# Which matrix products of a decoder block run as seven-product pairs, and which one runs beside the attention

## The chip, the cores and the metric

The kernel runs on one core of a Trainium2 chip. The metric is the device time of one execution in microseconds (us). Three runs of the kernel before gave a median of 1796.05 us (1795.31 to 1798.83). One further execution, 1795.55 us long, was recorded by the hardware profiler; every duration below comes from its trace.

## The reference

One layer of a hybrid decoder with S = 1024 tokens and D = 1024 channels, in float32. The parts that the change touches:

```
mod = silu(c) @ w_ada + b_ada                      # six rows of 1024: sh1, sc1, g1, sh2, sc2, g2
h = rms_norm(x, pre_norm1_w) * (1 + sc1) + sh1
z, xbc, dt_raw, q, k, v, gates = split(h @ w_in)   # 1024, 1536, 16, 1024, 1024, 1024, 2048 columns
y = ssd_chunked(silu(conv(xbc)), dt, ...) + d_skip * xs
y = y * silu(z)
y_ssd = y * rsqrt(mean of y*y over each of 2 groups of 512 channels + eps) * norm_w
q, k = partial_rope(q), partial_rope(k)            # 16 of each 64 channels are rotated by position
y_att = rms_norm(softmax1 @ v - lam * softmax2 @ v) per head, for 8 heads of 128 channels
gate_ssd, gate_att = split(sigmoid(gates))
merged = gate_ssd * (y_ssd @ w_ssd_o) + gate_att * (y_att @ w_attn_o)
x = x + g1 * rms_norm(merged @ w_out)
u = conv(h2 @ w_up);  x = x + g2 * rms_norm((gelu(u_gate) * u_val) @ w_down)
```

## The kernel before, in words

Everything is kept transposed, channels on the 128 partitions and tokens along the free axis. A float32 matrix product is done as three reduced-precision products: each operand is split into a high part (a copy on ScalarE, ACT) and a low part (the difference, on VectorE, DVE), and TensorE (PE) adds high·high, high·low and low·high. A *block* is 128 output channels of a projection for all 1024 tokens; with 8 slices of the input channels, 2 halves of the tokens and 3 products it takes 48 matmuls with a moving tile of 128x512.

Two blocks can also be made as a *pair*: the two blocks and the two halves of the tokens and of the input channels form a 2x2 product of matrices, done with seven products of sums instead of eight (`order`, `x_mms`, `x_split`, `x_sum`). A pair takes 7 x 4 x 3 = 84 matmuls where two blocks take 96. Its seven products gather in the PSUM banks X, Y, Z; DVE reads these into the result tiles `cg` and `cv` (`xcg`, `xcv` in the trace), and the work on a finished pair (`post(m, step)`) is laid over the time of the next pair by the table `steps_at`: at most one step after each of its seven products. Its weights arrive with `x_load` (SP's queue) in three buffers.

In the manual schedules the order of instructions on PE, DVE, ACT and SP is the order in which the code is written. SP issues nearly all the DMAs. The stages, in order:

1. The head: h, the first blocks of `xbc` and the first four blocks of gates.
2. The pairs loop: 13 pairs, listed in `pairs`: 2 of gates (`gs`, for gate_ssd), 6 that hold one q and one k block each (`qk` 2 to 7, heads that need no rotation in this layout), 5 of `xbc`. In the two pairs after the first, ten of the adaLN products are summed (`ada_sum`: DVE multiplies a 128x1024 tile of w_ada with silu(c) and sums along the row; three buffers `adas`).
3. z, also with seven products; six more `ada_sum`.
4. The SSD stage, units u = 0 to 15 of chunked recurrence; the blocks of v run between them as a dense stream (`fill`).
5. A stage called `seq`: four full blocks with rotation (`w_q` 0, `w_k` 0, `w_q` 1, `w_k` 1; `rope` does the rotation) and the eight blocks of the SSD output product (`w_ssd_o`; `so_half`, `so_out`), which also multiplies by the row `rsr` of 1/rms and by the gate. In the cover of this stage lie the split of y into `yT` (`split_y`), three `ada_sum`, and the differences of w_down that a later seven-product stage needs (`down_sum`, DVE, for k < KSO).
6. Attention: 64 items (8 heads j, 8 query blocks i). PE computes scores, transposes and values of an item; DVE the maxima, reciprocal and probabilities; ACT the exponentials. Item t's `transposes` on PE wait for its `probs` on DVE. To keep PE busy between, a dense stream is spread over the items by `fill(quota)`: 128 steps of three matmuls, the 8 blocks of gate_att (`gap`, tanh on ACT, a store to `gad`). `norm_o` normalises four query blocks of a head: POOL squares (`osb`), DVE reduces and scales (`sqt`), POOL takes the power -0.5 of `sqt` (`rstd_of`), DVE multiplies, POOL scales `osb`.
7. The attention output product, with the remaining `ada_sum`; `merged @ w_out`; the FFN up and down products.

The lists that set which blocks are made where:

```
pairs = [("gs", 4, 5), ("gs", 6, 7)] + [("qk", b, b) for b in range(2, 8)] + [("xbc", b, b + 1) for b in range(2, 12, 2)]
steps_at = {"gs": {0: (0,), 1: (4,)}, "qk": {0: (0, 1), 2: (4, 5)}, "xbc": {0: (0,), ..., 6: (7,)}}
seq = [("w_q", 0), ("w_k", 0), ("w_q", 1), ("w_k", 1)] + [("w_ssd_o", j) for j in range(8)] + [("w_gate", 8), ("w_gate", 9)]
```

## Time and profile before

| what | value |
|---|---|
| median of three runs | 1796.05 us (1795.31 to 1798.83) |
| the profiled execution | 1795.55 us, of which the span of the trace is 1793.8 us |
| PE busy | 1763.5 us, 98% of the span, 8563 matmuls |
| DVE, ACT, POOL busy | 1335.8 us (74%), 916.9 us (51%), 184.5 us (10%) |
| granted clock of PE | 0.999 |
| pairs loop | about 97 to 343 us |
| z | to about 395 us |
| SSD stage with v | 395 to 568 us |
| `seq` stage | 568 to 699 us |
| attention with the gate_att blocks | 699 to 959 us |

The lists of the profile are read so: a group of instructions has its line in the kernel, engine, operation, output and inputs by the program's names, shapes, count, then busy time in all and the mean of one in ns, then the idle time of that engine ahead of them and what ended it. A list of windows gives for each stretch the busy time and count on every engine, then the granted clock as a share of full speed, the busy share of the DMA engines and GB/s. A line of a timeline gives the start and the duration of one instruction, and in brackets how long its engine had been idle and who ended that.

### The profile page before, as it was taken

Reading aid. Unit: us, or ns where it says so; the run is one execution under the profiler, and the core shown is the slowest. Engines: PE = TensorE matmul, PEld = TensorE weight load, DVE = VectorE, ACT = ScalarE, POOL = GpSimd, SP = SyncE. Lnnn points to the kernel's source line nnn. Section 1 sums busy time; section 2 is a strip of 40 time slices with the busy share of each in tenths; the row PEclk is TensorE's granted clock in tenths of the full one; section 3 lists DMA queues with packets and bytes.
Section 4 is the critical chain, followed back from the end, with each engine's and each line's share of the span. In section 5 each row is a group of like instructions: output and inputs, shape, how many; then the busy total and the mean of one; then the engine's idle time right before and its main releaser. Section 6 shows DMA issues by size and latency. Waiting matters only on the chain.

```text
span 1793.8 us, 23879 instructions
## 1 busy us (share of the span) xinstructions
PE 1763.5 (98%) x8563; PEld 1456.3 (81%) x8563; DVE 1335.8 (74%) x2042; ACT 916.9 (51%) x1642; POOL 184.5 (10%) x189
## 2 busy tenths in 40 slices
PE   7999999999999999999999999999999999999998
PEld 4788888888878888888887888888888888888887
DVE  7887568864777787878876876688898888876545
ACT  7654445547765302666665232665454544554532
POOL 0000000002551300112122103100000000000001
PEclk9999999999999999999999999999999999999999
DMA  9465653356657798775728979212332232378744
GB/s 376 188 212 160 190 145 106 118 202 215 208 188 259 181 334 257 201 201 141 188 77 292 322 263 348 106 64 107 115 122 93 100 112 100 127 246 294 255 151 159
DMA packets 148330, 337.29 MB, mean 188 GB/s; under 512 B 15570, under 2 KB 50290, under 8 KB 148212
## 3 DMA queue, kind: packets, MB, share of 16 engines
q1 hardware_dynamic: 145012, 325.28, 55.4%
q0 software_dynamic: 3200, 10.49, 1.5%
q8 instruction: 67, 1.10, 0.3%
q14 instruction: 51, 0.42, 0.1%
HBM read 240.46 MB, written 95.25 MB: 187 GB/s over the span
## 4 chain that ended last, share of the span: by engine, by line
PE 56%; DVE 8%; DMA 3%; ACT 2%; issue 2%; POOL 1%; SPq 1%; DVEq 0%; POOLq 0%; ACTq 0%
PE upx L2043 4%; PE upx L2042 4%; PE upx L2044 4%; PE o L1700 2%; PE upy L2043 2%; PE upy L2042 2%; PE upy L2044 2%; PE dx L2438 2%; PE dx L2439 2%; PE dx L2437 2%; PE dy L2438 2%; PE dy L2437 2%; PE dy L2439 2%; PE mix L2116 2%; PE mix L2117 2%
## 5 line engine op out<-in xcount | busy, mean ns | idle before, releaser
L2042 PE MATMUL upx<-t,wu_t 128*128 128x512 f32 x264 | 103.1, 391 | 0.5 <-DVE cv L2502 0.4
L2043 PE MATMUL upx<-t,wu_t 128*128 128x512 f32 x264 | 102.8, 390 | 0.2 <-DVE t L2173 0.2
L2044 PE MATMUL upx<-t,wu_t 128*128 128x512 f32 x264 | 102.7, 389 | 0.0
L2016 ACT ACTIVATE wu_t<-sab 128x512 fp32r<-128x512 f32 x57 | 34.1, 627 | 127.7 <-DVE sab L2033 127.7
L102 DVE TENSOR_TENSOR g_lo<-gst,g_hi 128x1024 fp32r<-128x1024 f32 (+1 forms) x42 | 47.6, 1135 | 50.5 <-ACT g_hi L101 50.3
L1659 DVE CUSTOM_DVE_ANT_0 sc<-sc,mstrip 128x640 f32<-128x640 f32 (+3 forms) x64 | 65.9, 1029 | 14.4 <-PE sc L1626 13.9
L1671 ACT ACTIVATE p<-sc,nmx 128x640 f32<-128x640 f32 (+3 forms) x64 | 61.6, 962 | 28.3 <-DVE nmx L1659 24.6
L101 ACT ACTIVATE g_hi<-gst 128x1024 fp32r<-128x1024 f32 (+1 forms) x42 | 41.5, 989 | 67.0 <-DMA gst<-gld_s 35.4
L1700 PE MATMUL o<-vt,aT 128*128 128x128 f32 x576 | 74.8, 275 | 0.0
L1625 PE MATMUL sc<-kst,qst 128*128 128x512 f32 (+3 forms) x192 | 70.7, 373 | 2.9 <-ACT p L1671 2.6
L1700 PEld LDWEIGHTS o<-vt,aT 128*128 128x128 f32 x576 | 69.3, 192 | 0.6
L2561 POOL TENSOR_TENSOR rsf<-rsf,nhalf 128x1 f32<-128x1 f32 x8 | 5.2, 656 | 623.8 <-DVE rsf L2560 623.8
L1626 PE MATMUL sc<-klo,qst 128*128 128x512 f32 (+3 forms) x192 | 63.8, 341 | 0.0
L546 PE MATMUL xx<-xt,xw_t 128*128 128x512 f32 x156 | 61.0, 391 | 0.1
L2060 DVE SCALAR_TENSOR_TENSOR ug<-cg,vec,ug 128x1023 f32<-128x1023 f32 (+1 forms) x44 | 56.3, 1280 | 6.1 <-ACT ug L2059 5.3
L547 PE MATMUL xx<-xt,xw_t 128*128 128x512 f32 x156 | 60.7, 389 | 0.0
L548 PE MATMUL xx<-xt,xw_t 128*128 128x512 f32 x156 | 60.7, 389 | 0.0
L1690 ACT COPY aT<-at 128x512 f32<-128x512 f32 (+2 forms) x96 | 42.8, 482 | 33.3 <-PE at L1689 33.1
L2020 DVE TENSOR_TENSOR wu_t<-sab,wu_t 128x512 fp32r<-128x512 f32 x57 | 39.3, 690 | 26.6 <-ACT wu_t L2016 26.6
L2042 PEld LDWEIGHTS upx<-t,wu_t 128*128 128x128 f32 x264 | 49.6, 188 | 11.8 <-DVE cv L2502 1.4
L521 ACT ACTIVATE xw_t<-xsab 128x512 fp32r<-128x512 f32 x39 | 23.7, 627 | 67.5 <-DVE xsab L530 66.9
L2043 PEld LDWEIGHTS upx<-t,wu_t 128*128 128x128 f32 x264 | 49.6, 188 | 10.6 <-DVE t L2173 0.5
(580 smaller groups left out, 5735.6 us busy)
## 6 DMA issues: line engine op xcount, KB each, us to landing
adas<-in_w_ada SPq DMA_DIRECT2D x32, 512.0 KB
wuf<-in_w_up SPq DMA_DIRECT2D x22, 512.0 KB
gld_s<-gsum SPq DMA_DIRECT2D x22, 512.0 KB
gst<-gld_s SPq DMA_DIRECT2D x20, 512.0 KB
wdt_raw<-wtd SPq DMA_DIRECT2D x20, 512.0 KB
wuv<-in_w_up SPq DMA_DIRECT2D x19, 512.0 KB
gld_a<-ug SPq DMA_DIRECT2D x33, 256.0 KB
adat<-in_w_ada SPq DMA_DIRECT2D x16, 512.0 KB
```

The source lines that it names most:

```text
L546: T.matmul(o, wh, xh_, start=(k == 0 and first), stop=False, skip_group_check=not first)
L1625: T.matmul(sc, qs_[s][:, tsl], ks_[s][:, n0:n1], start=True, stop=False)
L1626: T.matmul(sc, qs_[s][:, tsl], kl[s][:, n0:n1], start=False, stop=True)
L1659: V.tensor_tensor_reduce(out=sc, in0=sc, in1=strip, scale=-1.0, scalar=BIG, op0=ALU.add, op1=ALU.min, accum_out=nmx[bq][s][:, 0:1])
L1671: A.activation(p.rearrange("p (h t) -> p h t", h=2) if i == 4 else p, sc, AF.Exp, scale=-1.0, bias=nmx[bq][s][:, 0:1], accum_out=ssum[bq][ ...
L1700: T.matmul(po_of[j, grp][:, qi, :], aTs[t % 2][:, kt // 4, kt % 4, :], vt[j % 2][:, kt, :], start=(kt == 0), stop=(kt == i))
L2042: T.matmul(out_, wh, xh_, start=(k == 0 and first), stop=False, skip_group_check=not first)
L2043: T.matmul(out_, wh, xl_, start=False, stop=False, skip_group_check=not first)
L2044: T.matmul(out_, wl, xh_, start=False, stop=(k == end), skip_group_check=not first)
L2437: T.matmul(o, gh[:, kk, tsl], wh, start=(k == 0 and not more), stop=False, skip_group_check=more)
L2438: T.matmul(o, gh[:, kk, tsl], wl, start=False, stop=False, skip_group_check=more)
L2439: T.matmul(o, gl[:, kk, tsl], wh, start=False, stop=(k == KF - 1), skip_group_check=more)
```

## The change

All sixteen gate blocks but the first four, and the rotated q and k blocks 0 and 1, become pairs: the list has 19 pairs instead of 13. The `seq` stage goes. The eight SSD output blocks become the dense stream of the attention, in place of the gate_att blocks, in 16 half blocks of 8 steps (128 steps as before); at each end ACT copies the bank, POOL multiplies by the loaded gate (`gtl`) and adds, and SP stores. The row `rsr` is now multiplied into y ahead of the split, on POOL (`scale_y`); half 0 of y is split at the end of the SSD stage, half 1 in the attention's items 5, 7, 9 and 11. All 32 `ada_sum` lie in the pairs (four in each gate pair but the first, two in each qk pair), in place and with two buffers. The first four k of `down_sum` go to POOL in attention items 16 to 47. The rotation's multiplication by `ropc` stays on POOL.

```diff
-    pairs = [("gs", 4, 5), ("gs", 6, 7)] + [("qk", b, b) for b in range(2, 8)] + [("xbc", b, b + 1) for b in range(2, 12, 2)]
+    pairs = [("gate", b, b + 1) for b in range(4, 16, 2)] + [("qk", b, b) for b in range(2, 8)] + [("rope", b, b) for b in range(2)] + [("xbc", b, b + 1) for b in range(2, 12, 2)]
...
+        elif kind == "rope":
+            w_ = ("w_q", "w_k")[n]
+            ropc, rops, sw, *his = rope_t
+            hi = his[n].bitcast(F32R)
+            if step % 4 == 0:
+                A.activation(c_, c_, AF.Copy, scale=qscale[w_])
+                V.stream_shuffle(sw, c_, perm)
+            elif step % 4 == 1:
+                G.tensor_tensor(c_, c_, ropc, op=ALU.mult)
+                V.tensor_tensor(sw, sw, rops, op=ALU.mult)
+            elif step % 4 == 2:
+                V.tensor_tensor(c_, c_, sw, op=ALU.add)
+                A.activation(hi, c_, AF.Copy)
+            else:
+                lo = c_.bitcast(F32R)
+                V.tensor_tensor(lo, c_, hi.bitcast(F32), op=ALU.subtract)
+                store_qk(w_, b, hi, lo)
...
+    steps_at = {"gate": {0: (0,), 1: (4,)}, ..., "rope": {0: (0,), 1: (1,), 2: (2,), 3: (3, 4), 4: (5,), 5: (6,), 6: (7,)}, "xbc": {...}}
...
-                    adas = [SL.get(f"adas{i}") for i in range(3)]
+                    adas = [SL.get(f"adas{i}") for i in range(2)]
...
-                if p < {1: 5, 2: 5}.get(m, 0):
-                    ada_sum(n_ald < 10)
+                if n_ada < 32 and p in {"gate": (1, 2, 3, 4), "qk": (1, 4)}.get(kind, ()) and m > 0:
+                    ada_sum()
...
+    def scale_y(half, kp):
+        t = yr_of[half, kp]
+        G.tensor_tensor(t, t, rsr[:, kp // 2 : kp // 2 + 1, :].broadcast_to([P, 2, HALF]), op=ALU.mult)
...
-    blocks = list(range(8))
+    blocks = [(j, 0) for j in range(4)] + [(j, 1) for j in range(4)] + [(j, h) for j in range(4, KD) for h in range(2)]
...
-                A.activation(gev[:, half, :], ps, AF.Tanh, scale=0.5)
-                SP.dma_start(gad[j][:, half * HALF : (half + 1) * HALF], gev[:, half, :])
+            e, g_ = gev[:, n % 2, :], gtl[:, n % 2, :]
+            A.copy(e, ps)
+            G.tensor_tensor(g_, g_, e, op=ALU.mult)
+            G.tensor_tensor(e, e, g_, op=ALU.add)
+            SP.dma_start(msd[j][:, hsl], e)
...
+            if t == 0:
+                norm_sums(ps_wc("norms")[:, : 2 * P], 1)
...
+            elif t == 2:
+                norm_rstd(1)
+                norm_row(1)
+            elif 4 <= t < 12:
+                kp = (t - 4) // 2
+                if t % 2 == 0:
+                    scale_y(1, kp)
+                else:
+                    for k in (2 * kp, 2 * kp + 1):
+                        split_y(k, 1)
...
+            elif 16 <= t < 48:
...
+                elif n in (3, 4, 5, 6):
+                    down_sum(wdr, k, n - 3, SP, G)
```

**The start of the attention.** On DVE the last rows of `so_out` (the gate times the SSD output) stood ahead of the first maxima (`sc`, `nmx`) before:

```order
L1461 TENSOR_TENSOR sev<-so_1_5658,rsr_5026 128x512 [waits DVE_49,PE_49]
L1461 TENSOR_TENSOR sev<-so_1_5658,rsr_5027 128x512
L1462 TENSOR_TENSOR sev<-sev 128x512 [waits DVE_49]
L1463 SCALAR_TENSOR_TENSOR gth_5071<-gth_5071,sev 128x512 [waits DVE_49]
L1653 TENSOR_TENSOR sc_0_0_5742<-sc_0_0_5742,maskneg 128x2x128 [waits PE_49]
L1654 TENSOR_REDUCE nmx_0_5711<-sc_0_0_5742 128x2 [waits DVE_49]
L1653 TENSOR_TENSOR sc_1_0_5747<-sc_1_0_5747,maskneg 128x2x128 [waits PE_49]
L1654 TENSOR_REDUCE nmx_0_5713<-sc_1_0_5747 128x2 [waits DVE_49]
```
Now the end of the SSD stage stands there: the last `tt` and `yt` of the recurrence, four splits of y (`yT`), the product of `yt` with silu(z) and the sum of squares, then the maxima, the first probabilities (`p`) and the low part of the weights of the dense stream's second block (`so_lo`):

```order
L1251 TENSOR_TENSOR tt<-po_1_5569,eb 128x512 [waits PE_49]
L1256 TENSOR_TENSOR yt_4286<-py_1_5575,yt_4286 128x512 [waits PE_49]
L1334 SCALAR_TENSOR_TENSOR yT_0_5594<-yr_5208,vec,yT_0_5594 128x512 [waits Activation_49]
L1334 SCALAR_TENSOR_TENSOR yT_0_5597<-yr_5208,vec,yT_0_5597 128x512 [waits Activation_49]
L1334 SCALAR_TENSOR_TENSOR yT_0_5600<-yr_5209,vec,yT_0_5600 128x512 [waits Activation_49]
L1334 SCALAR_TENSOR_TENSOR yT_0_5603<-yr_5209,vec,yT_0_5603 128x512 [waits Activation_49]
L1288 TENSOR_TENSOR yt_4286<-yt_4286,zt 128x1024 [waits DMAHW1_49,Pool_49]
L1282 TENSOR_REDUCE ssq<-zt 128x256 [waits Activation_49]
L1584 TENSOR_TENSOR sc_0_0_5667<-sc_0_0_5667,maskneg 128x2x128 [waits PE_49]
L1585 TENSOR_REDUCE nmx_0_5634<-sc_0_0_5667 128x2 [waits DVE_49]
L1584 TENSOR_TENSOR sc_1_0_5672<-sc_1_0_5672,maskneg 128x2x128 [waits PE_49]
L1585 TENSOR_REDUCE nmx_0_5636<-sc_1_0_5672 128x2 [waits DVE_49]
```
On ACT the last `vev` copy of v is followed by the high parts of these splits, the squares (`zt`), the exponentials, the copy of the first half block (`gev`), and only then the high part of the next weights (`so_hi`):

```order
L1198 COPY vev<-v_7_5540 128x512 [waits DMAHW6_49,PE_49]
L1333 ACTIVATE yT_0_5594<-yr_5208,vec 128x512 [waits Pool_49]
L1333 ACTIVATE yT_0_5597<-yr_5208,vec 128x512
L1333 ACTIVATE yT_0_5600<-yr_5209,vec 128x512 [waits Pool_49]
L1333 ACTIVATE yT_0_5603<-yr_5209,vec 128x512
L1279 ACTIVATE zt<-yt_4286 128x1024 [waits DMAHW1_49,DVE_49]
L1599 ACTIVATE p_0_5612,ssum_5632<-sc_0_0_5667,nmx_0_5634 128x128 [waits DVE_49,PE_49]
L1599 ACTIVATE p_0_5615,ssum_5632<-sc_0_0_5667,nmx_0_5634 128x128
L1599 ACTIVATE p_1_5613,ssum_5633<-sc_1_0_5672,nmx_0_5636 128x256 [waits DVE_49,PE_49]
L1599 ACTIVATE p_1_5616,ssum_5633<-sc_1_0_5672,nmx_0_5636 128x256
L1512 COPY gev<-sop_0_5660 128x512 [waits PE_49]
L1474 ACTIVATE so_hi<-so_raw 128x512 x2
```
What moved: the normalisation work that had the `seq` stage behind it now stands between the last unit of the SSD stage and the first items of the attention, on both engines.

**The rotation.** Before, DVE's rows of one rotated block stood in the `seq` stage among splits of weights (`w_k_lo`) and of y:

```order
L1391 STREAM_SHUFFLE sw<-qf 128x1024 [waits Activation_49]
L1393 TENSOR_TENSOR sw<-sw,rops 128x1024 [waits DMAHW1_49,DVE_49]
L1396 TENSOR_TENSOR qf<-qf,sw 128x1024 [waits DVE_49,Pool_49]
L1404 TENSOR_TENSOR thlo<-qf,thhi 128x1024 [waits Activation_49]
L1372 SCALAR_TENSOR_TENSOR yT_1_4883<-yr_4405,vec,yT_1_4883 128x512 [waits DMAHW0_49,Activation_49]
L1372 SCALAR_TENSOR_TENSOR yT_1_4886<-yr_4405,vec,yT_1_4886 128x512 [waits Activation_49]
L145 TENSOR_SCALAR rsn<-rsn 128x16 [waits DMAHW0_49]
L102 TENSOR_TENSOR w_k_lo<-w_k_raw,w_k_hi 128x1024 [waits DMAHW1_49,Activation_49]
L1391 STREAM_SHUFFLE sw<-qf 128x1024 [waits Activation_49]
L1393 TENSOR_TENSOR sw<-sw,rops 128x1024 [waits DVE_49]
L1372 SCALAR_TENSOR_TENSOR yT_1_4927<-yr_4406,vec,yT_1_4927 128x512 [waits DMAHW6_49,DMAHW2_49,Activation_49]
L1396 TENSOR_TENSOR qf<-qf,sw 128x1024 [waits DVE_49,Pool_49]
```
Now a rotated pair's rows stand among those of the next pair: its splits (`xw_t`, `xw_b`), the sums of its weights (`xsab`), and the reads of its banks (`xcg<-xz`, `xcv<-xx`):

```order
L617 STREAM_SHUFFLE sw<-xcg_942 128x1024 [waits Activation_49]
L529 TENSOR_TENSOR xsab_858<-xwf_2628,xwv_2726 128x512
L521 TENSOR_TENSOR xw_t_2880<-xsab_858,xw_t_2880 128x512 [waits Activation_49]
L620 TENSOR_TENSOR sw<-sw,rops 128x1024 [waits DMAHW7_49]
L857 TENSOR_TENSOR xcg_711<-xz_2846,xevs_941 128x512 [waits DMAHW2_49,DMAHW4_49,DMAHW0_49,PE_49]
L521 TENSOR_TENSOR xw_b_2900<-xsab_858,xw_b_2900 128x512 [waits Activation_49]
L622 TENSOR_TENSOR xcg_942<-xcg_942,sw 128x1024 [waits DVE_49,Pool_49]
L521 TENSOR_TENSOR xw_t_2919<-xwv_2726,xw_t_2919 128x512 [waits Activation_49]
L626 TENSOR_TENSOR xcg_942<-xcg_942,rhq 128x1024 [waits DVE_49]
L617 STREAM_SHUFFLE sw<-xcv_943 128x1024 [waits Activation_49]
L521 TENSOR_TENSOR xw_b_2956<-xwf_2782,xw_b_2956 128x512 [waits DMAHW5_49,Activation_49]
L620 TENSOR_TENSOR sw<-sw,rops 128x1024 [waits DVE_49]
```
What moved: the seven 128x1024 instructions of each rotated block (four on DVE, two on ACT, one on POOL) into the rhythm of the seven-product pairs.

**POOL in the attention.** Before, POOL had the three instructions of each `norm_o` in turn:

```order
L1708 TENSOR_TENSOR osb<-osb 128x512 [waits DMAHW3_49,Activation_49]
L146 TENSOR_TENSOR sqt<-sqt,nhalf 128x4 [waits DVE_49,Pool_49]
L1718 TENSOR_TENSOR osb<-osb,sqt 128x512 [waits DVE_49,PE_49]
L1708 TENSOR_TENSOR osb<-osb 128x512 [waits DMAHW5_49,Activation_49]
L146 TENSOR_TENSOR sqt<-sqt,nhalf 128x4 [waits DVE_49,Pool_49]
L1718 TENSOR_TENSOR osb<-osb,sqt 128x512 [waits DVE_49,PE_49]
```
Now the gate's product and sum (`gtl`, `gev`) and the differences of w_down (`wdr`) stand between them:

```order
L942 TENSOR_TENSOR wdr_6409<-wdr_6409 128x512 [waits DMAHW5_49]
L1513 TENSOR_TENSOR gtl<-gtl,gev 128x512 [waits DMAHW3_49,Activation_49]
L1514 TENSOR_TENSOR gev<-gev,gtl 128x512 [waits Pool_49]
L1639 TENSOR_TENSOR osb<-osb 128x512 [waits DMAHW7_49,Activation_49]
L942 TENSOR_TENSOR wdr_6409<-wdr_6410,wdr_6409 128x512 [waits DMAHW6_49]
L146 TENSOR_TENSOR sqt<-sqt,nhalf 128x4 [waits DVE_49]
L942 TENSOR_TENSOR wdr_6410<-wdr_6410,wdr_6409 128x512 [waits Pool_49]
L1649 TENSOR_TENSOR osb<-osb,sqt 128x512 [waits DVE_49,PE_49]
L942 TENSOR_TENSOR wdr_6410<-wdr_6410 128x512 [waits Pool_49]
L1639 TENSOR_TENSOR osb<-osb 128x512 [waits DMAHW4_49,Activation_49]
```
What moved: between the square of `osb` and the power of `sqt`, which DVE reads and waits for, POOL now has up to three other instructions.

447 lines of the change are left out of this document (177 added, 270 removed).

## The prediction, made before the run

> **What bounds the kernel now.** I read the page's busy times first, then the time by stage, then the waits of PE, and last the groups and timelines of the places that change.
>
> ```profile
> PE 1763.5 (98%) x8563; PEld 1456.3 (81%) x8563; DVE 1335.8 (74%) x2042; ACT 916.9 (51%) x1642; POOL 184.5 (10%) x189
> ```
>
> PE works 1763.5 of 1793.8 us; so a matmul less is time won, as long as nothing new makes PE wait. The windows show the stages (PE, weight loads, DVE, ACT, POOL busy us and counts, clock, DMA share, GB/s): a pair with five `ada_sum`, a qk pair, an xbc pair, the SSD stage, `seq`, attention.
>
> ```profile
> core 0: us, PE busy (x) PEld busy (x) DVE busy (x) ACT busy (x) POOL busy (x), PEclk, DMA share, GB/s
> 124.20:143.10 18.90, 18.83 (x83) 15.27 (x82) 17.14 (x34) 8.00 (x13) 0.00 (x0) 1.00 0.76 286
> 181.00:200.00 19.00, 19.00 (x85) 15.67 (x85) 12.45 (x18) 7.96 (x14) 0.00 (x0) 1.00 0.68 186
> 314.00:333.00 19.00, 19.00 (x85) 15.74 (x84) 16.09 (x21) 10.18 (x15) 0.00 (x0) 1.00 0.41 122
> 395.00:568.00 173.00, 172.51 (x1020) 138.09 (x1019) 108.21 (x152) 118.97 (x262) 68.68 (x56) 1.00 0.68 229
> 568.10:699.20 131.10, 130.04 (x577) 106.39 (x576) 101.21 (x132) 29.64 (x36) 17.86 (x7) 1.00 0.82 258
> 699.20:959.00 259.80, 252.48 (x1630) 220.86 (x1629) 204.01 (x477) 173.02 (x415) 52.75 (x50) 1.00 0.61 171
> ```
>
> PE is full in pairs, SSD stage and `seq` at full clock; only the attention has holes, 7.3 us of them, and DVE is at 79% there. The largest named holes hang on DVE's and ACT's work of an item:
>
> ```profile
> PE at L1689 <- DVE sqt L1717: 4.1, 8, 1.3
> PE sc L1625 <- ACT p L1671: 2.6, 6, 0.5
> ```
>
> **The gain.** The seven-product form takes 84 matmuls for 96. Removed is `seq`: 131.1 us for 576 matmuls, 0.2276 each. Added are six pairs (four of gates, two rotated) of 84; at 0.227 each, 19.07. Six make 114.4. The 384 matmuls of the SSD output replace the 384 of gate_att one for one in the attention. Gain 131.1 - 114.4 = 16.7 us, from 72 matmuls. That holds only where the work that had `seq`'s cover finds another.
>
> **Gate pairs and `ada_sum`: 0.3 us.** A gate pair adds a tanh, a store and four sums.
>
> ```profile
> L568 DVE SCALAR_TENSOR_TENSOR prod<-adas,srow 128x1024 f32<-128x1024 f32 x10 | 12.2, 1219 | 0.4 <-DMA adas<-in_w_ada 0.4
> ```
>
> DVE's own work of a pair is the qk pair's 12.45 less two low parts of q and k (128x1024, of the kind of `thlo` below, 1.22 each), so 10.0; with four sums of 1.22 it is 14.9 of 19.07. The window at 124.20 had five sums and 286 GB/s, and PE lost 0.07. The cover is the pair's PE time; two buffers instead of three could make a sum wait for its load, with the pair's own weight sums queued behind. I take 0.3 (0 to 1). The removed sums elsewhere lay beside PE work: 0.
>
> **Rotated pairs: 3.5 us (0 to 6.6).** Their seven instructions per block go into the next pair's time, at the prices of `seq`:
>
> ```profile
> L1391 DVE STREAM_SHUFFLE sw<-qf 128x1024 f32<-128x1024 f32 x4 | 5.3, 1328 | 0.0
> L1393 DVE TENSOR_TENSOR sw<-sw,rops 128x1024 f32<-128x1024 f32 x4 | 4.9, 1226 | 0.1
> L1396 DVE TENSOR_TENSOR qf<-qf,sw 128x1024 f32<-128x1024 f32 x4 | 4.9, 1222 | 6.9 <-POOL qf L1392 6.9
> L1404 DVE TENSOR_TENSOR thlo<-qf,thhi 128x1024 fp32r<-128x1024 f32 x4 | 4.9, 1220 | 1.1 <-ACT thhi L1401 1.1
> L1392 POOL TENSOR_TENSOR qf<-qf,ropc 128x1024 f32<-128x1024 f32 x4 | 13.0, 3248 | 32.4 <-DVE sw L1391 32.4
> ```
>
> DVE: 10.0 + 2 x (1.33 + 1.23 + 1.22 + 1.22) = 20.0 by durations. Instructions in a row overlap a little: below, one of 1.23 starts at 606.80 and the next at 607.95, 0.08 less. For some 24 instructions that is 1.9, so 18.1 of 19.07. DVE is nearly full, and its bank reads and splits have PE behind them. Then there is POOL:
>
> ```profile
> 606.80 1.23 DVE L1393 TENSOR_TENSOR sw<-sw,rops 128x1024 f32<-128x1024 f32 x1
> 607.95 2.88 DVE L1372 SCALAR_TENSOR_TENSOR yT<-yr,vec,yT 128x512 fp32r<-128x512 f32 x1
> 606.85 3.43 POOL L1392 TENSOR_TENSOR qf<-qf,ropc 128x1024 f32<-128x1024 f32 x1 [8.66 <-DVE sw L1391]
> L1372 DVE SCALAR_TENSOR_TENSOR yT<-yr,vec,yT 128x512 fp32r<-128x512 f32 x16 | 13.6, 880 | 4.5 <-ACT yT L1371 4.5
> ```
>
> A `yT` of 0.88 on the mean took 2.88 beside POOL's multiplication and ended just after it. If each of the four costs DVE about 2 us, that is 8.0, less 2 x 0.97 of slack: 6.1, and 0.5 for the 16 stores queued on SP ahead of weight loads: 6.6. If POOL runs beside instructions that it doesn't hold, 0. I take the middle, 3.5, since most of DVE's instructions there are of the kind that was held.
>
> **The start of the attention: 5.8 us (4 to 10).** The normalisation of the last SSD unit and the split of y had `seq` behind them; now the attention's first items are. The rows:
>
> ```profile
> L1371 ACT ACTIVATE yT<-yr,vec 128x512 fp32r<-128x512 f32 x16 | 10.6, 710 | 6.2 <-POOL yt L1245 4.2 <-DVE ssq L1267 2.1
> L1273 DVE TENSOR_TENSOR yt<-yt,zt 128x1024 f32<-128x1024 f32 x1 | 1.2, 1225 | 1.3 <-DMA zt<-zd 1.3
> L1264 ACT ACTIVATE zt<-yt 128x1024 f32<-128x1024 f32 x2 | 2.1, 1056 | 0.2 <-DVE yt L1273 0.2
> L1267 DVE TENSOR_REDUCE ssq<-zt 128x256 f32<-128x1024 f32 x2 | 4.0, 2008 | 0.5 <-ACT zt L1264 0.5
> L1553 ACT ACTIVATE ga_hi<-ga_raw 128x512 fp32r<-128x512 f32 x12 | 7.7, 639 | 0.0
> L1550 DVE TENSOR_TENSOR ga_lo<-ga_raw,ga_hi 128x512 fp32r<-128x512 f32 x12 | 8.5, 712 | 0.0
> 699.43 0.39 PE L1578 MATMUL gap<-hT,w_gate_hi 128*128 128x512 f32 x1
> 702.29 0.42 DVE L1653 TENSOR_TENSOR sc<-sc,maskneg 128x256 f32<-128x256 f32 x1
> 705.15 0.20 ACT L1668 ACTIVATION_READ_ACCUMULATOR p<-sc,nmx 128x1 f32 x1
> 706.02 0.60 ACT L1583 ACTIVATE gev<-gap 128x512 f32<-128x512 f32 x1 [0.66 <-PE gap L1580]
> ```
>
> Counted from the last matmul of v: ACT's copy of v (0.6) and four high parts of y (0.71 each, overlapping a little, so about 0.65 apart) end at 3.2, DVE's last low part at 4.0, yt times z at 5.2, the squares at 6.2, their sum at 8.2. From the first maxima to the last exponential of two items it took 702.29 to 705.35, 3.1: 11.3. Then the copy of the first half block (0.60), the high part (0.64) and the low part (0.71) of the second block's weights: 13.2. Meanwhile PE has the first 24 dense matmuls and the scores of two items, 6.6 by 699.43 to 706.02, and one more item's scores, about 0.8: 7.4. It then waits 5.8. Below this, 4, if v's last copies run ahead; above, 10, if `rsn`, which comes back through DRAM between items 0 and 2, keeps DVE waiting with maxima and `probs` behind it.
>
> **POOL and DVE in the attention: 4 us (1 to 10).** POOL gets 32 gate instructions, 16 `wdr` and four `scale_y`; DVE gets eight `yT` and loses nothing that bounds it.
>
> ```profile
> L1708 POOL TENSOR_TENSOR osb<-osb 128x512 f32<-128x512 f32 x15 | 15.6, 1042 | 123.7 <-ACT osb L1707 116.0 <-DMA atd<-osb 7.7
> L1273 DVE TENSOR_TENSOR yt<-yt,zt 128x1024 f32<-128x1024 f32 x8 | 10.8, 1354 | 1.3 <-DMA zt<-zd 1.3
> ```
>
> That is 48 x 1.04 + 4 x 3.25 = 63 us of POOL. How much DVE loses by it, the SSD stage shows: with 68.7 us of POOL in 173, the eight `yt` times z took 1354 ns on the mean against 1225 for the last, with POOL at rest. That is 10% of DVE's 108 us, 10 us for 69. For 63 it would be 9, and about a quarter lies where DVE bounds (once per head PE waits for DVE already, 8 times in the row above): 2.5. The second effect is POOL's queue:
>
> ```profile
> 839.24 1.01 POOL L146 TENSOR_TENSOR sqt<-sqt,nhalf 128x4 f32<-128x4 f32 x1 [1.88 <-DVE sqt L145]
> 840.87 0.15 DVE L1717 TENSOR_TENSOR sqt<-sqt,rsm 128x4 f32<-128x4 f32 x1
> ```
>
> The power ends at 840.25 and DVE's read of it starts at 840.87, 0.6 later. Where a gate's 2.1 us get in between, DVE stands up to 1.5 with `probs` behind; over some five places, mostly in short items with slack, 1. Two items with two `yT` each: 0.5. Sum 4; without any of it 1, and 10 if most of the 9 lands on the path.
>
> **End of the SSD stage: 0.5 us (0 to 2)**, four `scale_y` and four splits beside DVE at 108 and ACT at 119 of 173. The loads of the first heads and `down_sum` have a whole stage of cover: 0.
>
> **Sum.** -16.7 + 0.3 + 3.5 + 5.8 + 4 + 0.5 = -2.6. From 1795.55, the profiled execution, 1792.95; the median is 0.5 above it, so 1793.5.
>
> The Trainium skill ("SBUF — State Buffer", section "SBUF: two separate sides") speaks against this change: GpSimd and VectorE share a pair of ports as an exclusive lock, and a VectorE instruction with two SBUF inputs is blocked for the whole length of a GpSimd instruction that reads SBUF, or the reverse. The `yT` of 2.88 agrees; the SSD stage, where 69 us of POOL cost DVE some 10, shows that much of it falls where DVE idles. Taken at its word for all 63 us, the rule leads to the second rival.
>
> **Rivals.** (1) The covers hold and only the start is paid: -16.7 + 5.8 + 0.5 = -10.4, 1785.6. For it: PE lost nothing beside DVE at 17.14 of 18.90, and POOL cost the SSD stage no PE time. Against it: 18.1 of 19.07 before POOL is counted, and the attention's holes. Chance 0.28.
> (2) Slower, by POOL's hold on DVE: every POOL instruction in the rotated pairs and the attention keeps DVE from starting. Rotated pairs 6.6, attention 10, start 5.8, rest 0.8: +6.5, 1802.5. It turns the sign to slower by over 3.6 where the 52 added POOL instructions cost PE over 0.26 us each, 13.7 in all; I forecast 0.14. For it: the 2.88. Against it: most items have DVE idle time. Chance 0.18.
> (3) The change doesn't save: the added pairs run DMA-bound instead of at 19.07. The window with 286 GB/s and no loss speaks against it; at 1 us more for each of 14 gate, qk and rotated pairs the gain falls to about 3 and, with the other terms, the time is about 1807. Chance 0.03.
> The forecast, most of the gain spent, has 0.51.
>
> **The numbers.** 0.2%, 3.6 us, is about what a measurement of this kernel tells from no change: faster is below 1792.5, slower above 1799.6. The forecast's own range is 1789 to 1799; it gives 0.2 to faster, 0.29 to same, 0.02 to slower. The first rival gives 0.27 to faster, 0.01 to same; the second 0.03 to same and 0.15 to slower; the third 0.03 to slower. In all 0.47, 0.33 and 0.2. The range takes in the first rival and most of the second: 1784 to 1802.
>
> **What would show it.** Right: a hole of PE of 4 to 10 us just after v's last matmul, ended by `so_hi` or `so_lo`; in the two pairs after the rotated ones DVE over 95% busy, PE short of 19.07 by some us, and DVE instructions stretched beside `ropc`; the attention's idle PE time up from 7.3 to about 11; gate pairs at 19.1 each. Wrong: a start without the hole (DVE's order leaves PE other work), rotated pairs at full PE, or POOL instructions that stretch `probs` on every item.

## The result and the profile after: slower by 2.2%

The changed kernel took 1837.0 us (median of four runs, 1835.5 to 1838.1) against 1796.1 us for the kernel before (four runs, 1795.3 to 1798.8): a ratio of 1.0224, with a 95% interval of 1.0206 to 1.0242. It is 40.9 us slower where the forecast was 2.6 us faster; the time lies 35 us above the range. The span grew by 41.6 us, from 1793.8 to 1835.4.

Busy times and the longest waits of PE behind the head, from the page and the list of waits of the changed kernel (us in all, times, longest):

```profile
PE 1761.5 (96%) x8491; PEld 1450.5 (79%) x8491; DVE 1362.1 (74%) x2036; ACT 948.6 (52%) x1704; POOL 268.4 (15%) x245
```
```profile
PE sc L1556 <- ACT p L1602: 17.3, 10, 6.2
PE at L1620 <- DVE p L1612: 7.2, 10, 1.5
PE sc L1557 <- DMA klo<-kld: 6.9, 2, 6.4
PE xx L545 <- DVE xcv L869: 6.5, 3, 2.4
PE at L1620 <- DVE sqt L1648: 4.4, 7, 1.3
PE xx L545 <- ACT xevs L863: 3.6, 2, 3.0
PE pst L1268 <- DVE tt L1251: 2.9, 1, 2.9
```

The 72 matmuls are gone, as the counts show (8563 to 8491). PE's waits are longer: before, the largest of the named ones was 4.1. The first row (scores that wait for an exponential, because their bank is not yet read) was 2.6 before, with no wait over 0.5; the second (transposes that wait for the probabilities) was 0.3; the third (the low part of k, from DRAM) was not there.

Windows by stage of the changed kernel: a gate pair; 57 us over the two pairs that carry the rotations, which are the second rotated pair and the pair after it (three rows); z and the SSD stage with v; the start of the attention; its heads 0 and 1; its heads 2 to 7.

```profile
core 0: us, PE busy (x) PEld busy (x) DVE busy (x) ACT busy (x) POOL busy (x), PEclk, DMA share, GB/s
152.00:171.00 19.00, 19.00 (x85) 15.76 (x84) 15.49 (x32) 8.14 (x14) 0.00 (x0) 1.00 0.65 221
343.00:362.00 19.00, 18.43 (x82) 14.94 (x81) 15.05 (x19) 8.97 (x14) 4.21 (x2) 1.00 0.26 84
362.00:381.00 19.00, 14.40 (x63) 11.25 (x61) 16.81 (x19) 5.99 (x9) 3.92 (x2) 1.00 0.62 126
381.00:400.00 19.00, 15.72 (x61) 12.49 (x62) 16.22 (x19) 9.26 (x15) 2.73 (x1) 0.91 0.51 111
470.50:697.70 227.20, 223.78 (x1237) 180.00 (x1236) 142.64 (x183) 141.28 (x293) 77.73 (x61) 0.99 0.57 184
697.70:720.80 23.10, 14.73 (x62) 10.76 (x60) 13.81 (x22) 8.92 (x22) 5.49 (x5) 0.85 0.80 242
720.80:805.50 84.70, 68.22 (x402) 58.76 (x401) 65.17 (x126) 47.21 (x112) 29.26 (x21) 0.90 0.75 201
805.50:998.50 193.00, 180.50 (x1168) 156.67 (x1167) 163.14 (x343) 124.22 (x294) 89.28 (x74) 1.00 0.63 187
```

Gate pairs are full. Everything that had the cover of `seq` is not: the attention alone has 37.3 us without a matmul (8.4, 16.5 and 12.5 in the last three rows), 7.3 before. Measured between starts of matmuls, the stages of the two traces differ so (v's last matmul ends the SSD stage, the first of the dense stream ends `seq`, the first item's value product ends the start; "ideal" is 19.05 a pair):

| stage | before, us | after, us | difference | forecast |
|---|---|---|---|---|
| `seq` out, six ideal pairs in | 133.3 | 114.3 | -19.0 | -16.7 |
| first gate pair with sums | | | +1.6 | 0.3 |
| rotated pairs | | | +11.5 | 3.5 |
| z, SSD stage with v | 222.6 | 227.3 | +4.7 | 0.5 |
| start of the attention | 10.7 | 23.1 | +12.4 | 5.8 |
| attention, heads 0 and 1 | 62.9 | 84.7 | +21.8 | 4 with the next row |
| attention, heads 2 to 7 | 184.6 | 193.0 | +8.4 | |
| all else | | | +0.3 | 0 |

The gain came, and every cover that the change took away cost more than forecast. Nearly all of the +11.5 lies in the two pairs that carry the rotations: 22.6 and 26.7 us instead of 19.05 each.

**Rotated pairs.** Timeline of the changed kernel (start, duration, engine, instruction; in brackets the idle time before it and who ended that):

```profile
360.49 2.69 POOL L619 TENSOR_TENSOR xcv<-xcv,ropc 128x1024 f32<-128x1024 f32 x1 [9.37 <-DVE sw L617]
360.86 3.40 DVE L620 TENSOR_TENSOR sw<-sw,rops 128x1024 f32<-128x1024 f32 x1
364.18 0.68 DVE L869 TENSOR_TENSOR xcv<-xx,xevs 128x512 f32<-128x512 f32 x1
364.91 0.50 PE L545 MATMUL xx<-xt,xw_t 128*128 128x512 f32 x1 [2.42 <-DVE xcv L869]
```

`sw` takes 3.40 beside POOL's multiplication (1.21 where POOL rests) and PE stands 2.42 for the bank read queued behind it. The Trainium skill ("SBUF — State Buffer", section "SBUF: two separate sides") says that one of the two engines holds the shared port pair for the whole of its instruction; by that rule the trace agrees, 3.40 against 1.21.

**Start and first heads.** In the same trace, two stations of the start and the way of the second half of y to TensorE:

```profile
704.19 1.23 DVE L1288 TENSOR_TENSOR yt<-yt,zt 128x1024 f32<-128x1024 f32 x1 [2.01 <-DMA zt<-zd]
705.95 0.45 PE L1557 MATMUL sc<-klo,qst 128*128 128x128 f32 x1 [6.40 <-DMA klo<-kld]
716.65 0.50 PE L1508 MATMUL sop<-yT,so_lo 128*128 128x512 f32 x1 [0.65 <-DVE so_lo L1471]
```
```profile
745.42 2.34 POOL L1328 TENSOR_TENSOR yr<-yr,rsr 128x1024 f32<-128x1024 f32 x1 [5.43 <-DMA rsr<-rsd]
747.80 1.33 ACT L1333 ACTIVATE yT<-yr,vec 128x512 fp32r<-128x512 f32 x2 [4.06 <-POOL yr L1328]
748.55 1.42 DVE L1334 SCALAR_TENSOR_TENSOR yT<-yr,vec,yT 128x512 fp32r<-128x512 f32 x2 [4.68 <-ACT yT L1333]
749.88 1.23 DVE L1590 CUSTOM_DVE_ANT_0 sc<-sc,mstrip 128x1024 f32<-128x1024 f32 x1
752.52 0.58 PE L1556 MATMUL sc<-kst,qst 128*128 128x256 f32 x1 [6.21 <-ACT p L1602]
```

Read the second fence from the top: POOL waits for the row `rsr`, back through DRAM; ACT waits for POOL; DVE for ACT; the maxima of the next item (`sc`) stand behind on DVE; PE waits 6.21. One late row in DRAM stops four engines in turn, because ACT, DVE and PE do their instructions in the order written.

### The profile page after: what moved, and what is told of

Same layout as the page of the kernel before. It is cut to its first block, busy times and chain, and to the rows that moved or that the text cites. A ratio compares the mean times of both kernels' runs of the same rounds, so it can differ in the third digit from the quotient of the medians.

```text
span 1835.4 us, 23864 instructions
## 1 busy us (share of the span) xinstructions
PE 1761.5 (96%) x8491; PEld 1450.5 (79%) x8491; DVE 1362.1 (74%) x2036; ACT 948.6 (52%) x1704; POOL 268.4 (15%) x245
## 4 chain that ended last, share of the span: by engine, by line
PE 47%; DVE 8%; DMA 3%; ACT 2%; issue 2%; POOL 1%; SPq 0%; DVEq 0%; POOLq 0%; ACTq 0%
PE upx L1981 4%; PE upx L1980 4%; PE upx L1982 4%; PE upy L1980 2%; PE upy L1981 2%; PE upy L1982 2%; PE dx L2376 2%; PE dx L2377 2%; PE dx L2375 2%; PE o L1631 2%; PE dy L2375 2%; PE dy L2377 2%; PE dy L2376 2%; PE mix L2056 2%; PE mix L2054 2%; PE ao L123 2%
## 5 line engine op out<-in xcount | busy, mean ns | idle before, releaser
L545 PE MATMUL xx<-xt,xw_t 128*128 128x512 f32 x228 | 90.2, 396 | 10.1 <-DVE xcv L869 6.5
L1556 PE MATMUL sc<-kst,qst 128*128 128x512 f32 (+3 forms) x192 | 73.0, 385 | 17.7 <-ACT p L1602 17.3
L547 PE MATMUL xx<-xt,xw_t 128*128 128x512 f32 x228 | 89.4, 392 | 0.0
L546 PE MATMUL xx<-xt,xw_t 128*128 128x512 f32 x228 | 89.2, 391 | 0.0
L520 ACT ACTIVATE xw_t<-xsab 128x512 fp32r<-128x512 f32 x57 | 34.4, 627 | 90.9 <-DVE xsab L529 89.9
L101 ACT ACTIVATE g_hi<-gst 128x1024 fp32r<-128x1024 f32 (+1 forms) x42 | 41.6, 990 | 69.2 <-DMA gst<-gld_s 39.3
L521 DVE TENSOR_TENSOR xw_t<-xsab,xw_t 128x512 fp32r<-128x512 f32 x57 | 42.2, 740 | 35.1 <-ACT xw_t L520 35.1
L1612 DVE SCALAR_TENSOR_TENSOR p<-p,coef,p 128x128 f32<-128x128 f32 (+3 forms) x64 | 62.8, 982 | 2.3
L1556 PEld LDWEIGHTS sc<-kst,qst 128*128 128x128 f32 x192 | 37.3, 194 | 29.0 <-ACT p L1602 24.5
L1621 ACT COPY aT<-at 128x512 f32<-128x512 f32 (+2 forms) x96 | 42.7, 481 | 33.4 <-PE at L1620 33.3
```

The source lines that it names most:

```text
L545: T.matmul(o, wh, xh_, start=(k == 0 and first), stop=False, skip_group_check=not first)
L546: T.matmul(o, wh, xl_, start=False, stop=False, skip_group_check=not first)
L547: T.matmul(o, wl, xh_, start=False, stop=(k == KH - 1), skip_group_check=not first)
L1556: T.matmul(sc, qs_[s][:, tsl], ks_[s][:, n0:n1], start=True, stop=False)
```

## The experiments

Each kernel is the changed one with an edit. Each was run and profiled once, beside a run of the kernel before on the same chip (1794.6 to 1796.0 us); "saved" is against the changed kernel's 1837.0 us or its stage. What one execution can tell shows in the stages that an edit leaves alone: over the changed kernel and the experiments 1 to 11 that do not touch them, the two pairs that carry the rotations took 47.1 to 49.3 us together (49.3 in the changed kernel), z with the SSD stage 224.9 to 228.7, heads 0 and 1 82.5 to 85.2, heads 2 to 7 192.0 to 196.1. A smaller difference of a stage is not shown, and neither is one of 2 or 3 us of the whole time.

**1. The rotation's `ropc` on DVE.**

```diff
-                G.tensor_tensor(c_, c_, ropc, op=ALU.mult)
+                V.tensor_tensor(c_, c_, ropc, op=ALU.mult)
```

> The four multiplications by ropc go from POOL to DVE; nothing else changes. Theory A (POOL holds DVE): in the two pairs after the rotated ones PE loses 11 us now, because DVE's xw_t and sw stand 1.4 and 2.2 us longer beside POOL's 2.7; without POOL the pair has 20.5 us of DVE work for 19.07 of PE, so about 2 us a pair stay: some 7 us faster than the changed kernel, 1830, and no stretched xw_t or sw. Rival B (DVE is simply too full): 2.4 us of DVE more in each pair makes it about 5 us slower, 1842.

1834.9 us, between the two theories; the pairs took 371.9 us instead of 376.7. The two that carry the rotations took 45.1, where the kernels that leave them alone took 47.1 to 49.3. So POOL's hold is worth some 2 to 4 of the 11.5 us, and the greater part of the loss stays without POOL. No `sw` is stretched any more, though DVE has two more 128x1024 instructions in each of the two.

**2. High and low part of the rotated block one product later**, with the edit of 1.

```diff
-... "rope": {..., 3: (3, 4), 4: (5,), 5: (6,), 6: (7,)}
+... "rope": {..., 3: (3, 5), 4: (4, 6), 5: (7,), 6: (8, 9)}
```

> As rope_dve (no POOL in the rotated pairs), and ACT's high part of the rotated block stands one product later, so that ACT's copy of the bank (xevs), for which PE waited 2.8 us, no longer queues behind it; the low part one product later too. Theory A (ACT waiting in order for DVE's sum): pairs 371.9 us in rope_dve to about 368, 1831. Rival B (DVE full: 20.5 of 19.07): the wait moves to another bank, pairs 371 to 372, 1835.

1832.4 us, pairs 372.7 (45.7 in the two): nothing won there, as the rival said; the rest of the difference lies elsewhere in the trace. The wait for ACT is gone and DVE's is back, "PE xx" for `xcv`, 5.1 in 3. DVE's rows ahead of that bank read show why:

```profile
356.14 1.36 DVE L618 STREAM_SHUFFLE sw<-xcv 128x1024 f32<-128x1024 f32 x1
357.40 0.67 DVE L521 TENSOR_TENSOR xw_b<-xwf,xw_b 128x512 fp32r<-128x512 f32 x1
357.99 1.22 DVE L627 TENSOR_TENSOR xcg<-xcg,rhq 128x1024 fp32r<-128x1024 f32 x1
359.12 1.21 DVE L620 TENSOR_TENSOR xcv<-xcv,ropc 128x1024 f32<-128x1024 f32 x1
360.26 1.21 DVE L621 TENSOR_TENSOR sw<-sw,rops 128x1024 f32<-128x1024 f32 x1
361.39 0.68 DVE L870 TENSOR_TENSOR xcv<-xx,xevs 128x512 f32<-128x512 f32 x1
```

DVE works without a gap for 5.3 us and the read that PE waits for is last. In the same three windows of this kernel DVE is at most 91% busy; it is too slow only in the stretch ahead of the read.

**3. The loads of the first heads' q and k earlier**, ahead of the loads of y in the SSD stage; then **4. the same with ACT's queue** as `q`.

```diff
+                for n in range(2):
+                    SP.dma_start(qst[0][n].bitcast(F32), qd[n])
+                for t, n_, src in ((kst, "kst", khd), (klo, "klo", kld)):
+                    for n in range(2):
+                        load_k(n, t[0][n], src)
...
-                    SP.dma_start(qst[0][n].bitcast(F32), qd[n])
...
```
```diff
-            SP.dma_start(dst[64 * r : 64 * r + 64, :].bitcast(F32), src[m])
+            q.dma_start(dst[64 * r : 64 * r + 64, :].bitcast(F32), src[m])
```

> The loads of the first two heads' q and k are issued in SSD unit 12, ahead of the loads of y that wait for the normalisation, instead of in units 13 and 14; the slots are given in another order for it. Theory A (SP's queue): PE's waits for klo (6.9 us) go; what ends the hole then is the high part of the second block's weights behind the exponentials, so only 3 to 4 us are won: 1833, and the first transposes come 3 to 4 us earlier after v's end. Rival B (the transfers themselves are late because the DMA engines are full there): klo is still waited for, within 1 us of 1837.

> As heads_early, but the ten loads of the first heads are issued from ACT's queue instead of SP's. In heads_early PE's wait for klo went (start 18.6 instead of 23.1 us) and the SSD stage got 8.3 us longer, ACT waiting 9.5 us for the decay rows (M), whose load stood on SP behind the ten. Theory A (SP's queue): with the queue free the SSD stage comes back to 227 or less and the start stays at 19: 1832 or less. Rival B (the DMA engines are full, whatever the queue): the SSD stage stays over 232 us, 1837 or more.

1838.7 and 1840.8 us. In both, the start falls from 23.1 to 18.6, so the wait for `klo` is worth 4.5 there; and z with the SSD stage grows, from 227.3 to 235.6 and 235.7. A window near the end of that stage, of the first and then of the second:

```profile
670.00:680.00 10.00, 6.95 (x45) 5.14 (x44) 3.77 (x6) 6.31 (x15) 6.75 (x4) 1.00 1.04 330
```
```profile
670.00:680.00 10.00, 8.25 (x54) 6.59 (x52) 1.10 (x2) 0.00 (x0) 4.75 (x3) 1.00 1.04 337
```

The DMA engines are full (1.04, 330 and 337 GB/s), whichever queue issues the loads. What comes late in both is the load of the decay rows `M`: in the first, ACT stands 9.5 us for them and PE 5.9 behind; in the second, where SP has no such loads ahead of it, they still landed 9.4 us after their issue (median of two), and PE stands 11.0. In neither order has the end of the SSD stage room for what `seq` carried. In the second ACT also stood behind its own loads (14.7 us idle for one of them), so how much of its 11.0 is the DMA alone is not shown.

**5. The second half of y later**: power at item 4, scaling at 8, 10, 12, 14, split one item after, two buffers; **6. the same with the scaling on DVE.**

```diff
-            elif t == 2:
+            elif t == 4:
...
-            elif 4 <= t < 12:
-                kp = (t - 4) // 2
+            elif 8 <= t < 16:
+                kp = (t - 8) // 2
```
```diff
-                    scale_y(1, kp)
+                    scale_y(1, kp, V)
```

> In the attention the power of half 1's norms stands at item 4 instead of 2, scale_y at items 8, 10, 12, 14 and split_y at 9, 11, 13, 15, with two buffers for y instead of one, the next load right after the split before. POOL's work is the same. Theory A (the chain through DRAM, ACT and DVE waiting in order for scale_y): the losses of items 2, 5 and 9 (3.9, 7.2 and 6.8 us, 17.9 together) fall to 2 to 4: 14 to 16 us faster, 1822. Rival B (POOL's hold on DVE makes these losses): the same instructions in other items, at most 3 us faster, 1834 to 1837.

> As late_y, with the four scale_y of half 1 on DVE instead of POOL. late_y won 7.6 us in heads 0 and 1 where the chain alone gave 15; 14 us are still lost there. Theory A (what remains is POOL's hold: ACT and DVE wait in order for the scaled y, and DVE's small instructions are held for 2 us beside it): heads 0 and 1 fall from 77 to about 68 us, 1823. Rival B (what remains is the load of y and the order of the splits): 4 x 1.2 us more DVE, no gain, 1832 to 1835.

1832.0 and 1827.6 us; heads 0 and 1 took 77.1 and 73.9 instead of 84.7. The time that `rsr` gets is worth 7.6, half of what the first theory wanted. The scaling on DVE gives 3.2 more in these heads, little more than executions differ by; heads 2 to 7, which it leaves alone, took 196.1 in 6 and 193.6 in 5. PE's waits, in the order of the two kernels:

```profile
PE at L1620 <- DVE p L1612: 11.4, 11, 3.1
PE sc L1556 <- ACT p L1602: 6.9, 10, 1.1
```
```profile
PE sc L1556 <- ACT p L1602: 11.9, 10, 2.9
PE at L1620 <- DVE p L1612: 5.6, 8, 1.1
```

In 5 the long holes for the score banks (17.3, longest 6.2) become 6.9, and the waits for DVE's probabilities grow (7.2 to 11.4). In 6 these fall to 5.6, but the waits for the score banks are 11.9 again, in pieces of at most 2.9.

**7. Without the scaling of half 1** (its power, its row's way through DRAM and its four multiplications are left out; loads and splits stay); **8. without any of half 1's way** (loads and splits left out too; its blocks use half 0's parts).

```diff
-                norm_cols(1, False)
-            elif t == 2:
-                norm_rstd(1)
-                norm_row(1)
...
-                if t % 2 == 0:
-                    scale_y(1, kp)
-                else:
+                if t % 2 == 1:
```
```diff
-                if t % 2 == 0:
-                    scale_y(1, kp)
-                else:
-                    for k in (2 * kp, 2 * kp + 1):
-                        split_y(k, 1)
+                for k in range(KD):
+                    yT[k][1] = yT[k][0]
```

> Half 1 of y is split without its 1/rms (left out: the power, its way through DRAM and the four scale_y); splits and loads of y stay at their items. Theory A (the chain through DRAM and POOL's scaling together make the loss of heads 0 and 1): 84.7 us fall to 66 to 68, before it was 62.9: 1819. Rival B (the splits, their loads and the gates' work make most of it): over 75 us, 1828 or more.

> All of half 1's way in the attention is left out (power, round trip, loads of y, scaling and the eight splits; the half-1 blocks of the dense stream take half 0's split instead). In y_unscaled heads 0 and 1 still took 74.8 us where 62.9 stood before. Theory A (the splits on ACT and DVE in order behind the loads of y make that rest): heads 0 and 1 fall to 68 or less, the gate's 3.5 and the first wait staying: 1818. Rival B (head 1's loads and the gates make it): they stay over 72, 1823 or more.

1825.7 and 1816.9 us; heads 0 and 1 took 74.8 and 66.9. So of their 21.8 us, 9.9 are the scaling and its row, 7.9 the loads and splits of y, and 4.0 remain. Each cost alone was forecast near nothing ("Two items with two `yT` each: 0.5").

**9. The gate in one DVE instruction** from the bank, instead of ACT's copy and POOL's two; **10. that, and 16 of the w_down differences on POOL left out** (tiles are stored unchanged); **11. the gate's two POOL instructions left out** (the output product then enters without its gate).

```diff
-            A.copy(e, ps)
-            G.tensor_tensor(g_, g_, e, op=ALU.mult)
-            G.tensor_tensor(e, e, g_, op=ALU.add)
+            V.scalar_tensor_tensor(e, g_, 1.0, ps, op0=ALU.add, op1=ALU.mult)
```
```diff
-                    down_sum(wdr, k, n - 3, SP, G)
+                    SP.dma_start(wtd[...][:, k, (n - 3) // 2, :], wdr[(n - 3) // 2][:, (n - 3) % 2, :])
```
```diff
-            G.tensor_tensor(g_, g_, e, op=ALU.mult)
-            G.tensor_tensor(e, e, g_, op=ALU.add)
```

> At the end of each of the 16 half blocks one DVE instruction makes (gate + 1) times the PSUM bank, instead of ACT's copy and two POOL instructions. Theory A (POOL's hold and its queue cost the items): 32 POOL instructions of 1.04 to 1.6 us and 16 ACT copies go, 16 DVE instructions of 0.7 with only one operand in SBUF come: 4 to 6 us faster, 1832, of it most in heads 2 to 7, which lost 8.5. Rival B (DVE is the bound there, POOL beside it is nearly free): 11 us more DVE, a quarter of it on the path, 3 us slower, 1840.

> gate_psum, and the 16 differences of w_down for k = 0 to 3 are left out (the loaded tiles are stored unchanged, so that loads and stores stay). POOL then has norm_o and scale_y alone. Theory A (POOL's queue and hold make the 8 us that heads 2 to 7 lose): 193 us fall to 187 or less; with gate_psum's 5.6 the time is 1826. Rival B (something else there, the order of the dense stream or DMA): heads 2 to 7 stay at 192, 1831.

> The gate's product and sum on POOL are left out (the copied bank is stored as it is); the 16 differences of w_down, norm_o and scale_y stay on POOL. Theory A (the gate's 32 POOL instructions, by hold and queue, make the 8 us that heads 2 to 7 lose): 193 us fall to 187 or less. In pool_free DVE had taken the gate and waited for the bank in its own queue, which would explain why it won nothing there. Rival B (neither; the dense stream's other order of weights and blocks): heads 2 to 7 stay at 191 or more.

1831.4, 1833.7 and 1823.6 us. Heads 2 to 7 took 192.6, 192.6 and 185.2 (193.0 in the changed kernel, 184.6 before). From 800 to 950 us, one row for each of the changed kernel, 9, 10 and 11:

```profile
800.00:950.00 150.00, 140.55 (x901) 121.75 (x901) 128.32 (x268) 94.30 (x227) 69.20 (x57) 1.00 0.72 209
```
```profile
800.00:950.00 150.00, 141.02 (x906) 122.53 (x905) 122.06 (x281) 93.32 (x224) 51.04 (x44) 1.00 0.73 210
```
```profile
800.00:950.00 150.00, 141.15 (x906) 122.63 (x905) 118.19 (x278) 92.58 (x222) 27.88 (x28) 1.00 0.73 208
```
```profile
800.00:950.00 150.00, 145.25 (x946) 127.17 (x945) 124.20 (x284) 99.91 (x240) 52.01 (x45) 1.00 0.78 222
```

Taking 23 us of POOL away (the w_down differences, second to third row) changes nothing, though DVE is 3.9 us less busy: POOL's work there lies where DVE has slack. Taking the gate's work away gives 7.8 of the 8.4 us, and 45 matmuls more in the same 150 us. Moved to DVE it costs the same. So POOL's total is not what costs there; the gate's work is, on either engine.

The waits show two ways. In heads 2 to 7 PE waits 5.7 us for DVE's probabilities in the changed kernel (0.3 before), and 7.3 for the score banks in 9 (2.3 before and in 11). On POOL the gate holds DVE, as in this place of the changed kernel, where a `p` of 128x384 takes 1.70 (0.62 in 11):

```profile
838.85 1.26 POOL L1514 TENSOR_TENSOR gev<-gev,gtl 128x512 f32<-128x512 f32 x1
838.82 1.70 DVE L1612 SCALAR_TENSOR_TENSOR p<-p,coef,p 128x384 f32<-128x384 f32 x1
840.67 0.52 PE L1620 MATMUL at<-ident,p 128*128 128x128 f32 x3 [1.48 <-DVE p L1612]
```

On DVE the gate's instruction stands in DVE's own queue until the block's last matmul is done: in 9 DVE is idle for it 13 times, 23.3 us in all, with the next item's maxima behind. One of these rows:

```profile
830.94 0.69 DVE L1512 SCALAR_TENSOR_TENSOR gev<-gtl,sop 128x512 f32<-128x512 f32 x1 [2.03 <-PE sop L1508]
```

In 9, heads 0 and 1 gained 4.4, in 11 they gained 3.5.

**12. The good edits together**: 2, 6 and 9.

```diff
+... "rope": {..., 3: (3, 5), 4: (4, 6), 5: (7,), 6: (8, 9)}
+            elif 8 <= t < 16: ... scale_y(1, kp, V)
+            V.scalar_tensor_tensor(e, g_, 1.0, ps, op0=ALU.add, op1=ALU.mult)
```

> late_y_dve, rope2 and gate_psum together. Alone they won 9.4, 4.6 and 5.6 us. If they are separate places: 1837 - 19.6 = 1817; if they share waits, 1821 or more.

1819.5 us: 17.5 saved of 19.6. By stage the edits do not add so well: heads 0 and 1 took 73.4, where 6 alone had 73.9, so 9's 4.4 is not seen there; 2.4 came in the start, which none of the three edits was for, and 5.3 in the pairs. The start (20.7, before 10.7), the first heads (33.4 and 40.0, before 31.6 and 31.3), heads 2 to 7 (193.4, before 184.6) and what is left in the rotated pairs keep it some 24 us above the kernel before.

**13. A cover given back**: gate blocks 12 to 15 as four full blocks between the SSD stage and the attention, with the normalisation, the loads of the heads and the splits of y below them, and four sums of the adaLN in each qk pair. **14. That, with 2 and 9** added. **15. The cover of 13 with six sums** in a gate pair and two or three in a qk pair (the first change of the second diff); the buffers of the blocks' results are also handed on later. **16. That, with 2 and 9** and with the blocks' weights fetched one block earlier (its second).

```diff
-    pairs = [("gate", b, b + 1) for b in range(4, 16, 2)] + ...
+    pairs = [("gate", b, b + 1) for b in range(4, 12, 2)] + ...
+    seq = [("w_gate", b) for b in range(12, 16)] + [("w_ssd_o", 0), ("w_ssd_o", 1)]
+    for n in range(4):
...
+            block_half(ps[:, half, :], seq_w[n], hT, half)
...
```
```diff
-{"gate": (1, 2, 3, 4), "qk": (1, 2, 3, 4)}
+{"gate": (0, 1, 2, 3, 4, 5), "qk": (1, 3, 4) if i_ > 5 else (1, 4)}
...
-                    fetch_seq(n + 2)
+                    fetch_seq(n + 3)
```

> Two of the six gate pairs are undone: gate blocks 12 to 15 run as four full blocks (192 matmuls, 43.7 us instead of 38.1) between the SSD stage and the attention. Under them lie the split of half 0, the loads of the first heads, the norms of half 1, its scaling and half of its split; the rest of the split is at items 1 and 3. The ada_sum of the two pairs go to the qk pairs. Theory A (the change's loss is the cover of the normalisation that went with the seq stage): the start after v or the blocks falls from 23 to about 11 us, heads 0 and 1 from 85 to 65, the SSD stage's 4 us come back; with 5.6 for the matmuls 1837 - 12 - 20 - 4 + 5.6 = 1806. Rival B (POOL's gates and w_down differences in the attention make the loss; they are all still there): heads 0 and 1 stay over 75, 1818 or more.

> cover4, rope2 and gate_psum together. If the three causes are separate places, their gains add: 1806 - 6 (rotated pairs) - 4 (the gate's work in the heads) = 1796, level with the kernel before. If the stages only hand their waits on, as heads_early did, it stays above 1801.

> cover4 again with two of its side effects taken out: the ada_sum of the undone pairs stand in the gate pairs (six each; two qk pairs have three) instead of four in each qk pair, where SP's queue is full of stores of q and k; and the buffers of the gate blocks' results are handed on last, since an exponential of the second item waited 4 us for one of them. Theory A (lost cover): pairs 355 to about 340 us, the start 65 to 61, SSD end 223.6 and heads 0 and 1 71 as in cover4: 1837 - 16 = 1821. Rival B (the cover gives back what it costs): above 1832.

> cover4b with the weights of the four gate blocks and of the first SSD output block loaded one block earlier (their load had stood on SP behind the round trip of half 1's norms and PE waited for its high part), with rope2 and gate_psum. Theory A (separate places): 1825 - 3 (the load) - 4 (rotated pairs) - 3 (gates) = 1815. Rival B (the waits are shared): 1820 or more. Either way it stays behind the kernel before, since the two rotated pairs alone, the gates of heads 2 to 7 and the start keep over 20 us.

1839.2, 1839.0, 1825.0 and 1822.4 us. The cover does what it should at the attention, where heads 0 and 1 took 71.1 in 13 and 69.4 in 15, and for the end of the SSD stage, 223.6 (222.6 before). In 13 it lost that in the pairs: the sums waited for their loads, behind the stores of q and k on SP.

```profile
PE xx L545 <- DVE xcv L869: 18.4, 7, 5.0
```
```profile
227.82 1.23 DVE L567 SCALAR_TENSOR_TENSOR adas<-adas,srow 128x1024 f32<-128x1024 f32 x1 [3.96 <-DMA adas<-in_w_ada]
```

15 took these 14.7 us back (pairs 355.4 to 340.7). Its start stays at 64.3, of which the four blocks are about 44, so some 20 us of start are left behind a cover of 44, where 10.7 stood before; what makes them was not tested (PE's longest holes there are 3.0 for the probabilities and 1.6 for the first weights). 14 and 16 gave less than the sum of their parts; where they share a wait was not taken apart.

## Why the prediction was wrong

The gain came as forecast; what failed is the price of the lost cover, in every term of it and most of all in the attention (4 forecast, 30.2 measured).

- **The gain** was right: six added pairs at 19.05, gate pairs full. It was 19.0 and not 16.7, mostly because the window for `seq` began 1.7 us after the stage's first matmul. The first pair with sums lost 1.6 where 0.3 was given.
- **"The loads of the first heads and `down_sum` have a whole stage of cover: 0."** This failed for the loads. Those of the first heads (3 MB for q and k) are issued from 686.67 us on, 11 us before v's last matmul and among the loads of y; the stage's mean DMA share in the prediction's own window, 0.68, does not show these units. 3 and 4 show 1.04 there: the start was relieved of 4.5 us only by giving 8.3 to 8.4 to the stage before. `down_sum` itself did cost nothing (10).
- **The end of the SSD stage, 0.5**, was 4.7, for another reason than these loads, which are issued after its hole. ACT waits for the decay rows `M`, and PE for DVE behind it (2.9 in the list above, at 680.76, with 1.6 of half clock after it):

```profile
SPq L1309 <- POOL rsn L146: 4.3, 1, 4.3
675.71 1.29 ACT L999 ACTIVATE eb<-M 64x512 f32<-64x512 f32 x2 [5.21 <-DMA M<-acd]
```

  SP had stood 4.3 us for POOL's power of half 0's norms, with the load of `M` behind, and the DMA share from 670 to 680 us is 0.94. In 15 SP stands the same 4.3, yet the stage takes 223.6, so the round trip alone does not make the loss; no experiment took the two apart.
- **The start, 5.8**, was 12.4, and its mechanism was another: `so_hi` and `so_lo` end 0.5 and 0.65 of it, as the order said, but the hole that counts is 6.4 for `klo`, a transfer. It was worked out from engine durations alone. `zt`, also a late load, has `yt` start 2.0 after DVE is free.
- **POOL and DVE in the attention, 4 (1 to 10)**, was 30.2. This is the largest miss, in two parts. The first heads: y's way into the first items was costed by its instructions (0.5, and for two items where the change has four), not by what is queued behind them; 7 and 8 measure 9.9 for scaling and row and 7.9 for loads and splits. The upper bound of the start's term did name `rsr` with "maxima and `probs` behind it", but at 4 us in all. The later heads: 3.5 was given for POOL's hold and POOL's queue, and 11 takes out 7.8 by the gate alone. The hold is the part that grew (PE's wait for `p`, 0.3 to 5.7); the wait for `sqt`, which POOL's queue was to lengthen, did not (3.2 before, 3.4 after). The w_down differences cost nothing (10).
- **Rotated pairs, 3.5 (0 to 6.6)**, was 11.5. POOL's part was some 2 to 4, inside the range. What was left out is the order in DVE's queue: the mean (18.1 of 19.07 then, at most 88% of a window now, not the 95% that was to show it) does not show that a bank read stands behind 5.3 us of work (2).
- **The rivals.** The second had the sign, at 1802.5, and part of the cause: POOL's hold is shown in the rotated pairs and by the gate in heads 2 to 7, and with the round trip it is in the 9.9 of y. The loads, the row in DRAM and the order in the queues were in none of the three rivals. The first needed covers that hold.
- **What was in no term: the granted clock.** The last section has it: at most 11.8 us of the 41.6.

If the causes are separate places, heads 0 and 1 are accounted for by 17.8 (y) and 3.5 (gate), 21.3 of 21.8, the part at half clock lying inside these; 12 warns that they are not quite separate. Of the start 6.9 is `klo` (both waits), 1.2 the weights, 2.5 the clock; some 1.8 was not taken apart, and no kernel that moves the last unit's normalisation behind the first items was run. No version here beats the kernel before.
